# Hybrid decoder layer: the mLSTM convolutions placed with the output gate's units, and the last two pairs of down sums moved into the down projection

## The chip, the cores and the metric

The kernel runs on one core of one Trainium2 chip. The metric is the device time of one execution in microseconds (us), as the median over runs. The engines are PE (matmuls), DVE, ACT, POOL (elementwise work) and SP, whose queue issues nearly all transfers between HBM and on-chip memory. Each engine takes its instructions in the order in which they were written into its stream, and stands still at one whose operands are not there.

## The reference

One layer of a decoder trunk in float32, sequence 1024, width 1024. One input projection feeds a differential-attention group and an mLSTM group; their outputs go through an output projection; a gated MLP (inner width 2816) with a width-3 convolution follows.

```python
hn = rmsnorm(x, attn_norm_w)
da_q, da_k, da_v, ml_qk, ml_v, ml_o, ml_i, ml_f = split_projection(hn @ w_in)
...
qk = silu(causal_dwconv(ml_qk, mlstm_conv_w, mlstm_conv_b))      # width 4, 1024 channels
mq, mk = split(qk)
i_pre, logf = ml_i + igate_b, log_sigmoid(ml_f + fgate_b)
h = rmsnorm(mlstm_chunkwise(mq, mk * 128 ** -0.5, ml_v, i_pre, logf))
ml_out = sigmoid(ml_o) * h
x = x + concat([da_out, ml_out]) @ w_out
u = causal_dwconv(rmsnorm(x) @ w_up, ffn_conv_w, ffn_conv_b)
gate, up = split(u)
x = x + (silu(gate) * up) @ w_down
out = rmsnorm(x)
```

## The kernel before

**Arithmetic.** Every float32 matrix is split into a high and a low part: ACT copies it rounded (L112), DVE or POOL subtracts that from the source (L113, the same shape). A product is then three matmuls (L155 to L157 with moving x, L160 to L162 with moving weights). Up and down projections are done by a scheme that uses seven products of half-size blocks instead of eight, with sums of blocks as operands.

**First projections.** Eight column tiles `ct` of the convolved half (mq is 0 to 3, mk 4 to 7) are projected first, each in two halves of 512 positions. A half ends with ACT's copy out of PSUM (L376, L390) into `mqk`, and DVE multiplies the whole tile by the norm's row `RB` (L384, L391). `conv_qk(ct)` makes the width-4 convolution: one ACT instruction (L358) and three DVE instructions of some 1,022 columns (L360), into a tile tagged `ta` (four buffers). `silu_qk(ct)` is one ACT instruction (L363). Behind the column tiles PE does the gate projection, 16 matmuls per half (L408), each half in a PSUM bank tagged `sa` or `sb` and copied out by DVE (L409). Then come the output gate's units, `o_unit(tt)`, 24 matmuls for 128 positions each with the four pieces of weights `wo`, and the same with `wv` in `v_unit(tt)`, mixed with the small work on the gates (L474 transposes them).

**Down sums.** The seven-product scheme needs sums of blocks of `w_down`. They depend on weights alone, so they are made early: `down_sums` loads a pair of row blocks, POOL makes four subtractions of 128x512 in place (L324), and `store_sums` writes the pair to `wsum` in HBM (L330). There are 11 pairs. `late_sums` does the same in the `ta` tiles. Two pairs of up sums follow in `first_up_sums`.

**Down projection.** PE makes 77 steps, seven products (order 1, 2, 7, 5, 6, 4, 3) of 11 steps i, 12 matmuls a step. Ahead of step k `dprep_to(k + 5)` prepares operands: some products need sums of activation blocks (L1153, DVE), each step needs two splits, one of activations (`hb`, `a`) and one of weights (tiles `wf` and `bw`, loaded two steps at a time, from `w_down` in products 1, 2 and 3 and from `wsum` in 7, 5, 6 and 4). A finished product is added into the `x2` tiles (L1194, DVE). `fill(k)` issues the loads that belong to step k: activation blocks `a21`, `a12`, `a22`, the residual tiles `x2[0..3]` at steps 8 to 11 and `x2[4..7]` at 20 to 26, and the final norm's row `fin` at 19.

**Order.** The text of the program is not the order of an engine. A scheduler places each instruction by when its inputs are expected, so two texts can give one order, and a load can move ahead of others on SP. SP has one queue: a store that waits for POOL holds up the weights behind it.

Of the kernel before, what the change touches and what calls it, by code (L numbers as in the profile page):

```python
# [13 lines left out]
AF = mybir.ActivationFunctionType  # L14
ALU = mybir.AluOpType
# [9 lines left out]
NJ = DFF // P  # L25
# [14 lines left out]
def tile_hybrid(ctx: ExitStack, tc: tile.TileContext, I: dict, out: bass.AP):  # L40
    nc = tc.nc
    V = nc.vector
    A = nc.scalar
    PE = nc.tensor
    GP = nc.gpsimd
# [61 lines left out]
    wsum = dp.tile([NJ // 2, 2, P, 1024], F32, name="wsum")  # L107
# [13 lines left out]
    HV = (slice(0, 512), slice(512, 1024))  # L121
# [50 lines left out]
    def small(shape):  # L172

        flip[0] ^= 1
        return psA.t(shape, tag="sa" if flip[0] else "sb")
# [7 lines left out]
    def rotate(n):  # L183
        return (mmps, lambda: big([P, 512]), lambda: small([P, 512]))[n % 3]()
# [12 lines left out]
    def load_x(i, hf, between=None):  # L197
        f = pa.t(XS, tag="ta", bufs=4)
        for c in ([slice(0, 1), slice(1, 2)] if between else [slice(0, 2)]):
            nc.sync.dma_start(f[:, c, :], I["xT"][:, 2 * i + c.start:2 * i + c.stop, HV[hf]])  # L200
            if between and c.start == 0:
                between()
        return f
# [41 lines left out]
    def col_piece(ct):  # L245
        cw[ct, 0], cw[ct, 1] = wpiece(I["w_st"][ct], None, V)

    g0 = col_halves(0, 0, 1, first=True)
    f = load_x(0, 0, lambda: next(g0))
    next(g0)  # L250
    split_x(0, 0, f)
    f = load_x(1, 0)
# [5 lines left out]
    f = load_x(2, 0)  # L258
# [3 lines left out]
    f = load_x(3, 0)  # L262
# [5 lines left out]
    for i in range(4):  # L268
        f = load_x(i, 1)
# [39 lines left out]
    gs = pa.t([16, S], tag="gs")  # L309
# [1 line left out]


    dsum = []
    pairs = list(range(NJ // 2))

    def down_sums(alloc=lambda: pr0.t([P, S], tag="vda", bufs=4), n=1):
        h0, h1 = HV
        for i in (pairs.pop(0) for _ in range(min(n, len(pairs)))):
            g, u = (alloc() for _ in range(2))
            for k, f in enumerate((g, u)):  # L320
                nc.sync.dma_start(f, I["w_down"][2 * i + k])
            for dst, x_, y in ((g[:, h1], g[:, h1], g[:, h0]), (u[:, h1], u[:, h1], g[:, h1]),
                               (u[:, h0], u[:, h0], u[:, h1]), (g[:, h0], u[:, h1], g[:, h0])):
                GP.tensor_tensor(dst, x_, y, op=ALU.subtract)  # L324
            dsum.append((i, g, u))

    def store_sums(n=1):
        for i, g, u in (dsum.pop(0) for _ in range(min(n, len(dsum)))):
            for k, f in enumerate((g, u)):
                nc.sync.dma_start(usum[i - NJ, k] if i >= NJ else wsum[i, k], f)  # L330
# [13 lines left out]
    def tok(tiles, tt):  # L344
        return tiles[tt // 2][:, tt % 2, :]

    def col_mm(ps, ct, kc, hf):
        k = slice(kc % 4 * P, (kc % 4 + 1) * P)
        w = cw[ct, kc // 4]
        mm3(ps, w[:, 0, k], w[:, 1, k], *xpart(kc, hf), kc == 0, kc == KC - 1)  # L350
# [3 lines left out]
    def conv_qk(ct):  # L354

        u = M[ct]
        acc = cacc[ct] = pa.t([P, S], tag="ta", bufs=4)
        A.activation(acc, u, AF.Identity, bias=mcb[:, ct:ct + 1], scale=mcw[:, ct, 3:4])  # L358
        for d in (1, 2, 3):
            V.scalar_tensor_tensor(acc[:, d:], u[:, :S - d], mcw[:, ct, 3 - d:4 - d], acc[:, d:], op0=ALU.mult, op1=ALU.add)  # L360

    def silu_qk(ct):
        A.activation(M[ct], cacc.pop(ct), AF.Silu)  # L363
# [21 lines left out]
    for ct in range(4, 8):  # L385
        for hf in range(2):
            ps = rotate(2 * ct + hf)
            for kc in range(KC):
                col_mm(ps, ct, kc, hf)
            A.activation(M[ct][:, HV[hf]], ps, AF.Copy)  # L390
        V.tensor_tensor(M[ct], M[ct], RB, op=ALU.mult)  # L391
        store_sums()
        down_sums()
        if ct == 4:
            col_piece(7)
        elif ct == 6:
            wo = [getw(0) for _ in range(4)]
        conv_qk(ct - 4)
        if ct > 4:
            silu_qk(ct - 5)  # L400
    mq, mk = M[0:4], M[4:8]


    for hf in range(2):
        gp = small([16, 512])
        for kc in range(KC):
            for m, x_ in enumerate(xpart(kc, hf)):
                PE.matmul(gp, wg16[:, kc, :], x_, start=(kc, m) == (0, 0), stop=(kc, m) == (KC - 1, 1))  # L408
        V.tensor_copy(gs[:, HV[hf]], gp)  # L409
    conv_qk(4)  # L410
    silu_qk(3)

    def mv_mm(ps, w, tt):
        for kc in range(KC):
# [6 lines left out]
    def late_sums():  # L421
        store_sums()
        down_sums(lambda: pa.t([P, S], tag="ta", bufs=4))
# [7 lines left out]

    def o_unit(tt):
        store_sums()
        if tt < 4:
            if tt < 3:
                conv_qk(5 + tt)
            silu_qk(4 + tt)
        if tt % 2:
            late_sums()
        if tt == 5:  # L440
            wv.extend(getw(0) for _ in range(4))
        if tt == NT - 1:
            return
        tts = (tt,) if tt < NT - 2 else (tt, tt + 1)
        pss = [rotate(k) for k in tts]
        mv_pair(pss, wo, tts)
        for ps, k in zip(pss, tts):
            A.activation(tok(Tt, k), ps, AF.Tanh, scale=rstdh[:, k:k + 1])

    def v_unit(tt):  # L450
        store_sums()
        if tt in (2, 4):
            first_up_sums(tt // 2 - 1)
        if tt == 0:
            late_sums()
            vda.extend(pr0.t([P, 2, 512], tag="vda", bufs=4) for _ in range(4))
        if tt == NT - 1:
            return
        tts = (tt,) if tt < NT - 2 else (tt, tt + 1)
        pss = [rotate(k + 2) for k in tts]  # L460
        mv_pair(pss, wv, tts)
        for ps, k in zip(pss, tts):
            A.activation(tok(vda, k), ps, AF.Copy, scale=rstd[:, k:k + 1])
# [325 lines left out]
    x2 = []  # L789
# [326 lines left out]
    def weights(p, i):  # L1116
        if i % 2 == 0:
            wload(p, i)
        return wb.pop((p, i))

    def fill(k):

        if k == 2:
            load(a21[:, 0:4, :], "A21", (0, 4))
        elif k == 4:
            load(a12, "A12", (4, NP - 1))
        elif k == 6:
            load(a21[:, 4:8, :], "A21", (4, 8))
        elif k in (8, 9, 10, 11):
            nc.sync.dma_start(x2[k - 8], x2d[k - 8])  # L1130
        elif k == 12:
            load(a21[:, 8:, :], "A21", (8, NP))
            load(a12[:, NP - 5:, :], "A12", (NP - 1, NP))
        elif k == 13:
            load(a22[:, 0:6, :], "A22", (0, 6))
        elif k == 17:
            load(a22[:, 6:, :], "A22", (6, NP))
        elif k in (20, 22, 24, 26):
            tt = 4 + (k - 20) // 2
            nc.sync.dma_start(x2[tt], x2d[tt])  # L1140
        elif k == 19:
            nc.sync.dma_start(fin, I["final_norm"].partition_broadcast(P))
            V.tensor_scalar(fin, fin, RSC, None, op0=ALU.mult)
# [40 lines left out]
    x2 = [pd.t([P, D], tag="x2", bufs=8) for _ in range(NT)]  # L1184
# [69 lines left out]
    k = 0  # L1254
# [95 lines left out]
```

## Time and profile before

| quantity | value |
|---|---|
| median of 3 runs | 1224.06 us (1218.65 to 1227.42) |
| the profiled execution's own time | 1228.44 us |
| its span in the profile | 1226.6 us |
| busy PE, DVE, ACT, POOL | 1196.3, 898.2, 572.6, 475.5 us |
| mean granted PE clock | 0.994 |
| down projection, first matmul | 1006.64 us |

Times in the profile count from the span's start; 1.8 us of the execution lie outside the span. `PEclk` or "granted clock" is the share of full speed that PE was granted. A row of a timeline gives start, duration, engine, line, operation, output and input tiles, shape, count, and in brackets the idle time ahead of it with what ended it.

### The profile page before, as it was taken

Reading aid. Unit: us, or ns where it says so; the run is one execution under the profiler, and the core shown is the slowest. Engines: PE = TensorE matmul, PEld = TensorE weight load, DVE = VectorE, ACT = ScalarE, POOL = GpSimd, SP = SyncE. Lnnn points to the kernel's source line nnn. Section 1 sums busy time; section 2 is a strip of 40 time slices with the busy share of each in tenths; the row PEclk is TensorE's granted clock in tenths of the full one; section 3 lists DMA queues with packets and bytes.
Section 4 is the critical chain, followed back from the end, with each engine's and each line's share of the span. In section 5 each row is a group of like instructions: output and inputs, shape, how many; then the busy total and the mean of one; then the engine's idle time right before and its main releaser. Section 6 shows DMA issues by size and latency. Waiting matters only on the chain.

```text
span 1226.6 us, 15935 instructions
## 1 busy us (share of the span) xinstructions
PE 1196.3 (98%) x5622; PEld 977.0 (80%) x5622; DVE 898.2 (73%) x1564; ACT 572.6 (47%) x1114; POOL 475.5 (39%) x364
## 2 busy tenths in 40 slices
PE   9998999999999999999999999999999999999996
PEld 7885788888778878888888888888888888888885
DVE  5598232566767777669998878787787768896694
ACT  6533323333666665444643443434344445544462
POOL 0475441003543431001398878786877600000000
PEclk9998999999999999999999999999999999999999
DMA  8755564114212252432222222222222158832323
GB/s 304 257 207 196 216 240 164 61 70 158 75 54 51 69 167 100 138 129 99 99 69 103 86 102 70 86 69 86 80 76 101 54 207 321 308 106 96 95 78 137
DMA packets 61744, 159.03 MB, mean 130 GB/s; under 512 B 6177, under 2 KB 10465, under 8 KB 61665
## 3 DMA queue, kind: packets, MB, share of 16 engines
q1 hardware_dynamic: 61232, 157.21, 37.3%
q8 instruction: 44, 0.72, 0.2%
q10 hardware_dynamic: 432, 0.82, 0.2%
q14 instruction: 36, 0.29, 0.1%
HBM read 116.02 MB, written 37.78 MB: 125 GB/s over the span
## 4 chain that ended last, share of the span: by engine, by line
PE 80%; DMA 5%; DVE 5%; ACT 3%; POOL 3%; issue 2%; SPq 1%; POOLq 0%; ACTq 0%; DVEq 0%
PE mm L155 6%; PE mm L157 6%; PE mm L156 5%; PE mm L160 5%; PE mm L162 4%; PE mm L161 4%; PE big L155 4%; PE big L157 4%; PE big L156 4%; PE big L160 4%; PE big L162 4%; PE big L161 4%; PE sb L769 3%; POOL vda L324 3%; PE sb L155 2%
## 5 line engine op out<-in xcount | busy, mean ns | idle before, releaser
L112 ACT ACTIVATE w<-wf 128x512 fp32r<-128x512 f32 x160 | 97.8, 624 | 137.4 <-PE mm L157 33.7
L113 DVE TENSOR_TENSOR w<-wf,w 128x512 fp32r<-128x512 f32 x128 | 109.6, 868 | 24.1 <-ACT w L112 18.7
L1033 DVE SCALAR_TENSOR_TENSOR y<-x2b,fcw,y 128x1022 f32<-128x1022 f32 x44 | 89.6, 2076 | 0.0
L1032 DVE SCALAR_TENSOR_TENSOR y<-x2b,fcw,y 128x1023 f32<-128x1023 f32 x44 | 71.3, 1660 | 10.4 <-ACT y L1031 10.4
L324 POOL TENSOR_TENSOR vda<-vda 128x512 f32<-128x512 f32 x24 | 47.1, 1978 | 63.3 <-DMA vda<-in_w_down_dram 62.4
L113 POOL TENSOR_TENSOR w<-s,w 128x512 fp32r<-128x512 f32 x40 | 68.3, 1706 | 7.1 <-ACT w L112 7.1
L113 POOL TENSOR_TENSOR w<-wf,w 128x512 fp32r<-128x512 f32 x32 | 46.2, 1449 | 62.4 <-ACT w L112 50.2
L113 POOL TENSOR_TENSOR w<-wu,w 128x512 fp32r<-128x512 f32 x40 | 67.4, 1685 | 2.9 <-ACT w L112 2.9
L155 PE MATMUL mm<-xb,w 128*128 128x512 f32 x168 | 66.4, 395 | 0.0
L157 PE MATMUL mm<-xb,w 128*128 128x512 f32 x168 | 65.9, 392 | 0.0
L156 PE MATMUL mm<-xb,w 128*128 128x512 f32 x168 | 65.9, 392 | 0.0
L744 DVE CUSTOM_DVE_ANT_0 s<-big,B 128x128 f32<-128x128 f32 (+7 forms) x64 | 47.6, 754 | 14.0 <-PE big L742 12.6
L1031 ACT ACTIVATE y<-x2b,fcw 128x1024 f32<-128x1024 f32 x44 | 52.3, 1237 | 11.2 <-DVE x2b L1022 9.8
L746 ACT ACTIVATE s<-s,mb 128x128 f32<-128x128 f32 (+7 forms) x64 | 49.3, 772 | 11.5 <-DVE mb L745 10.4
L112 ACT ACTIVATE w<-s 128x512 fp32r<-128x512 f32 x43 | 27.0, 629 | 55.1 <-PE mm L157 18.6
L160 PE MATMUL big<-w 128*128 128x512 f32 x132 | 51.5, 390 | 0.8 <-DVE x L1194 0.8
L960 POOL TENSOR_TENSOR s<-wu 128x512 f32<-128x512 f32 x20 | 31.2, 1562 | 54.2 <-DMA wu<-in_w_up_dram 54.2
L162 PE MATMUL big<-w 128*128 128x512 f32 x132 | 51.4, 389 | 0.0
L161 PE MATMUL big<-w 128*128 128x512 f32 x132 | 51.4, 389 | 0.0
L112 ACT ACTIVATE w<-wu 128x512 fp32r<-128x512 f32 x48 | 29.8, 627 | 43.6 <-PE mm L157 13.4
L1022 DVE TENSOR_TENSOR x2b<-x2b,big 128x512 f32<-128x512 f32 x53 | 35.4, 680 | 20.0 <-PE big L157 19.2
L1022 DVE TENSOR_TENSOR x2b<-x2b,mm 128x512 f32<-128x512 f32 x51 | 34.1, 681 | 21.4 <-PE mm L157 20.6
(514 smaller groups left out, 3802.0 us busy)
## 6 DMA issues: line engine op xcount, KB each, us to landing
wf<-in_w_up_dram SPq DMA_DIRECT2D x22, 512.0 KB, 4.4
actd<-y SPq DMA_DIRECT2D x21, 512.0 KB, 2.6
wu<-in_w_up_dram SPq DMA_DIRECT2D x20, 512.0 KB, 3.5
wf<-in_w_st_dram SPq DMA_DIRECT2D x12, 512.0 KB, 4.2
vda<-in_w_down_dram SPq DMA_DIRECT2D x12, 512.0 KB, 5.9
wsum<-vda SPq DMA_DIRECT2D x12, 512.0 KB, 3.1
wf<-in_w_mv_dram SPq DMA_DIRECT2D x12, 512.0 KB, 5.3
wf<-wsum SPq DMA_DIRECT2D x12, 512.0 KB, 3.4
```

Of the source, the lines that this page charges most:

```text
L112: A.activation(dst[:, 0, :], src, AF.Copy)
L113: loeng.tensor_tensor(dst[:, 1, :], src, dst[:, 0, :].bitcast(F32), op=ALU.subtract)
L155: PE.matmul(ps, sh, mh, start=first, stop=False)
L156: PE.matmul(ps, sh, ml, start=False, stop=False)
L157: PE.matmul(ps, sl, mh, start=False, stop=last)
L160: PE.matmul(ps, sh, w[:, 0, :], start=first, stop=False)
L161: PE.matmul(ps, sl, w[:, 0, :], start=False, stop=False)
L162: PE.matmul(ps, sh, w[:, 1, :], start=False, stop=last)
L324: GP.tensor_tensor(dst, x_, y, op=ALU.subtract)
L1022: V.tensor_tensor(dst, src, ps, op=ALU.add)
L1032: V.scalar_tensor_tensor(y[:, 1:], u[:, :S - 1], cw[:, 1:2], y[:, 1:], op0=ALU.mult, op1=ALU.add)
L1033: V.scalar_tensor_tensor(y[:, 2:], u[:, :S - 2], cw[:, 0:1], y[:, 2:], op0=ALU.mult, op1=ALU.add)
```

## The change

Three things move.

The first projections make down sums in `ct` 5 and 7 only (besides 1 and 3 of the first half), and the convolutions stand one tile to three tiles later in the text: tile `ct - 5` in the loop, tiles 3 to 7 in `o_unit(0..4)`. The gates are copied out of PSUM by ACT instead of DVE.

The two last pairs of down sums (9 and 10) leave the first projections. `fill` makes them in the down projection: at steps 14 and 15 it loads them into the tiles of `x2[4..7]`, POOL subtracts, at steps 18 and 20 they are stored to `wsum`, and the residual is loaded into those tiles two steps later than before. Product 7, the first that reads `wsum`, begins at step 22; its pair 8 and 9 is loaded for step 30.

`late_sums` in the v units moves from unit 0 to 2, and the up sums from 2 and 4 to 3 and 5.

```diff
-    pairs = list(range(NJ // 2))
+    pairs = list(range(NJ // 2 - 2))
+
+    def pair_sums(g, u):
+        h0, h1 = HV
+        for dst, x_, y in ((g[:, h1], g[:, h1], g[:, h0]), (u[:, h1], u[:, h1], g[:, h1]),
+                           (u[:, h0], u[:, h0], u[:, h1]), (g[:, h0], u[:, h1], g[:, h0])):
+            GP.tensor_tensor(dst, x_, y, op=ALU.subtract)
...
         V.tensor_tensor(M[ct], M[ct], RB, op=ALU.mult)
-        store_sums()
-        down_sums()
+        if ct % 2:
+            store_sums()
+            down_sums()
...
-        conv_qk(ct - 4)
         if ct > 4:
-            silu_qk(ct - 5)
+            conv_qk(ct - 5)
+        if ct > 5:
+            silu_qk(ct - 6)
...
-        V.tensor_copy(gs[:, HV[hf]], gp)
-    conv_qk(4)
-    silu_qk(3)
+        A.activation(gs[:, HV[hf]], gp, AF.Copy)
...
     def o_unit(tt):
         store_sums()
-        if tt < 4:
-            if tt < 3:
-                conv_qk(5 + tt)
-            silu_qk(4 + tt)
         if tt % 2:
             late_sums()
+        if tt < 5:
+            conv_qk(3 + tt)
+        if tt < 6:
+            silu_qk(2 + tt)
...
+    def last_sums(i, g, u):
+
+        for m, f in enumerate((g, u)):
+            nc.sync.dma_start(f, I["w_down"][2 * i + m])
+        pair_sums(g, u)
+
     def fill(k):
...
+        elif k in (14, 15):
+            last_sums(k - 5, x2[2 * k - 24], x2[2 * k - 23])
+        elif k in (18, 20):
+            i = k // 2
+            for m in range(2):
+                nc.sync.dma_start(wsum[i, m], x2[2 * i - 14 + m])
-        elif k in (20, 22, 24, 26):
-            tt = 4 + (k - 20) // 2
+        elif k in (22, 24, 26, 28):
+            tt = 4 + (k - 22) // 2
             nc.sync.dma_start(x2[tt], x2d[tt])
```

**SP in the first projections.** These are the rows of SP's queue from the weights of column tile 7 (`wf<-in_w_st`) to the last two of the four `wo` loads (`wf<-in_w_mv`); `vda` and `ta` loads are pairs of down sums, two rows a pair, and `wsum<-vda` stores one. Before:

```order
L126 DMA wf<-in_w_st_dram 128x1024
L330 DMA wsum<-vda 128x1024 x2
L321 DMA vda<-in_w_down_dram 128x1024 x4
L330 DMA wsum<-vda 128x1024 x2
L126 DMA wf<-in_w_mv_dram 128x1024 x2
L330 DMA wsum<-vda 128x1024 x2
L126 DMA wf<-in_w_mv_dram 128x1024 x2
```

Now, over the same stretch:

```order
L126 DMA wf<-in_w_st_dram 128x1024
L326 DMA vda<-in_w_down_dram 128x1024
L333 DMA wsum<-vda 128x1024 x2
L326 DMA vda<-in_w_down_dram 128x1024
L126 DMA wf<-in_w_mv_dram 128x1024 x2
L333 DMA wsum<-vda 128x1024 x2
L326 DMA vda<-in_w_down_dram 128x1024 x2
L126 DMA wf<-in_w_mv_dram 128x1024
L326 DMA ta<-in_w_down_dram 128x1024
L333 DMA wsum<-vda 128x1024 x2
L326 DMA ta<-in_w_down_dram 128x1024
L126 DMA wf<-in_w_mv_dram 128x1024
```

The first two `wo` loads stand behind the stores of pairs 0 and 1 instead of 0 to 3, the third behind 0 to 2 and the fourth behind 0 to 3, instead of 0 to 4 for both.

**ACT around the gate projection.** The rows from the second half of column tile 6 on (`mqk_254` is that tile, `mqk_253` and `mqk_255` the ones beside it; `sa` is the PSUM bank that the gates' second half needs). Before:

```order
L390 ACTIVATE mqk_254<-big_718 128x512
L112 ACTIVATE w_776<-wf_771 128x512
L363 ACTIVATE mqk_253<-ta_906 128x1024
L358 ACTIVATE ta_938<-mqk_254,par_67 128x1024
L390 ACTIVATE mqk_255<-sa_793 128x512
L363 ACTIVATE mqk_254<-ta_938 128x1024
L112 ACTIVATE w_781<-wf_779 128x512
L112 ACTIVATE w_784<-wf_779 128x512
L390 ACTIVATE mqk_255<-mm_819 128x512
L358 ACTIVATE ta_1003<-mqk_255,par_67 128x1024
L363 ACTIVATE mqk_255<-ta_1003 128x1024
```

Now:

```order
L393 ACTIVATE mqk_254<-big_702 128x512
L112 ACTIVATE w_750<-wf_745 128x512
L366 ACTIVATE mqk_253<-ta_971 128x1024
L361 ACTIVATE ta_1011<-mqk_254,par_67 128x1024
L393 ACTIVATE mqk_255<-sa_767 128x512
L366 ACTIVATE mqk_254<-ta_1011 128x1024
L112 ACTIVATE w_755<-wf_753 128x512
L112 ACTIVATE w_758<-wf_753 128x512
L393 ACTIVATE mqk_255<-mm_793 128x512
L361 ACTIVATE ta_1045<-mqk_255,par_67 128x1024
L414 ACTIVATE gs_260<-sb_836 16x512
L414 ACTIVATE gs_260<-sa_854 16x512
```

The order is the same up to the two gate copies, which are new on ACT and stand ahead of the last silu. On DVE the 24 convolution instructions also still stand ahead of the first work on the gates, and 18 of them ahead of the product of `mqk_254` with `RB`, as before.

**DVE in the down projection, second product.** The rows from step 19 on (`w2_9173` and `w2_9174` are its two splits before, `w2_9159` and `w2_9160` now; `a21<-a21,a22` is a block sum). Before:

```order
L113 TENSOR_TENSOR w2_9173<-a12_8828,w2_9173 128x512
L113 TENSOR_TENSOR w_9194<-a12_8828,w_9194 128x512
L1153 TENSOR_TENSOR a21_8829<-a21_8829,a22_8830 128x512 x4
L113 TENSOR_TENSOR w2_9174<-wf_9175,w2_9174 128x512
L113 TENSOR_TENSOR w_9195<-wf_9175,w_9195 128x512
L113 TENSOR_TENSOR w_9213<-a12_8828,w_9213 128x512
L113 TENSOR_TENSOR w_9214<-bw_9215,w_9214 128x512
L113 TENSOR_TENSOR w_9235<-hb_8707,w_9235 128x512
L1153 TENSOR_TENSOR a21_8829<-a21_8829,a22_8830 128x512 x6
L113 TENSOR_TENSOR w_9236<-wf_9237,w_9236 128x512
```

Now (from the third row on):

```order
L1169 TENSOR_TENSOR a21_8809<-a21_8809,a22_8810 128x512 x6
L113 TENSOR_TENSOR w2_9160<-wf_9161,w2_9160 128x512
L113 TENSOR_TENSOR w_9187<-wf_9161,w_9187 128x512
L113 TENSOR_TENSOR w_9205<-a12_8808,w_9205 128x512
L113 TENSOR_TENSOR w_9206<-bw_9207,w_9206 128x512
L113 TENSOR_TENSOR w_9227<-hb_8687,w_9227 128x512
L113 TENSOR_TENSOR w2_9271<-hb_8687,w2_9271 128x512
L1169 TENSOR_TENSOR hb_8687<-a22_8810,hb_8687 128x512 x2
L1210 TENSOR_TENSOR x2_8811<-x2_8811,mm_9060 128x512
L1210 TENSOR_TENSOR x2_8812<-x2_8812,mm_9061 128x512
L1210 TENSOR_TENSOR x2_8813<-x2_8813,sb_9062 128x512
L1210 TENSOR_TENSOR x2_8814<-x2_8814,sa_9063 128x512
```

Six block sums instead of four stand ahead of step 19's weights, and the four additions of the finished second product stand ahead of `w_9228`, step 22's weights, which follow them by one block sum (`w_9236` is the same split before). On SP the four new loads (L1128) stand between the first load of `a22` and its second one, the weights of steps 19 and 20 behind the first two of them and those of step 21 behind all four; the stores (L1153) stand behind step 22's weights, two ahead of `fin`, two ahead of the weights of step 26.

More of the change, by code (lines that the diff above doesn't have):

```diff
@@ L313, in tile_hybrid @@
     dsum = []
-    pairs = list(range(NJ // 2))
+    pairs = list(range(NJ // 2 - 2))
[4 more added lines that the diff above has]
+            GP.tensor_tensor(dst, x_, y, op=ALU.subtract)
     def down_sums(alloc=lambda: pr0.t([P, S], tag="vda", bufs=4), n=1):
-        h0, h1 = HV
         for i in (pairs.pop(0) for _ in range(min(n, len(pairs)))):
@@ L321, in down_sums @@
                 nc.sync.dma_start(f, I["w_down"][2 * i + k])
-            for dst, x_, y in ((g[:, h1], g[:, h1], g[:, h0]), (u[:, h1], u[:, h1], g[:, h1]),
-                               (u[:, h0], u[:, h0], u[:, h1]), (g[:, h0], u[:, h1], g[:, h0])):
-                GP.tensor_tensor(dst, x_, y, op=ALU.subtract)
+            pair_sums(g, u)
             dsum.append((i, g, u))
@@ L451, in v_unit @@
         store_sums()
-        if tt in (2, 4):
+        if tt == 2:
+            late_sums()
+        if tt in (3, 5):
             first_up_sums(tt // 2 - 1)
         if tt == 0:
-            late_sums()
             vda.extend(pr0.t([P, 2, 512], tag="vda", bufs=4) for _ in range(4))
@@ L1119, in weights @@
         return wb.pop((p, i))
+    def last_sums(i, g, u):
+        for m, f in enumerate((g, u)):
+            nc.sync.dma_start(f, I["w_down"][2 * i + m])
+        pair_sums(g, u)
     def fill(k):
```

## The prediction

> **What bounds the kernel now.** I read the engine table first, then the waits of PE, then stretches of time around them.
>
> ```profile
> PE 1196.3 (98%) x5622; PEld 977.0 (80%) x5622; DVE 898.2 (73%) x1564; ACT 572.6 (47%) x1114; POOL 475.5 (39%) x364
> ...
> PE sa L408 <- ACT mqk L390: 5.9, 1, 5.9
> ...
> PE big L600 <- DVE kw L597: 3.1, 3, 1.4
> ...
> PE sb L474 <- DVE gs L409: 2.5, 1, 2.5
> ```
>
> PE is busy for all but 30 us of 1226.6, so an edit off PE is worth only a PE wait that it removes or makes. The first and third wait are the ones this change can reach: the gate projection (L408) waits for a PSUM bank that ACT empties late, and the gates' transposes (L474) wait for DVE's copy of them. Their stretch in PE's timeline and in windows (columns: length, busy PE, PEld, DVE, ACT, POOL, granted clock, DMA share, GB/s):
>
> ```profile
> 96.12 3.87 PE L408 MATMUL sb<-xb,wg 128*16 128x512 f32 x16
> 105.94 5.57 PE L408 MATMUL sa<-xb,wg 128*16 128x512 f32 x16 [5.94 <-ACT mqk L390]
> ...
> 106.00:110.00 4.00, 4.00 (x11) 1.33 (x12) 3.96 (x2) 0.00 (x0) 3.92 (x3) 0.54 0.00 0
> ...
> 122.00:126.00 4.00, 1.49 (x12) 0.99 (x11) 3.46 (x4) 1.30 (x2) 1.53 (x1) 1.00 0.78 271
> 126.00:130.00 4.00, 4.00 (x13) 3.11 (x12) 0.95 (x6) 3.94 (x6) 1.37 (x2) 0.59 0.98 362
> ```
>
> The first wait costs 5.94 us, and the same sixteen matmuls then take 5.57 us instead of 3.87: 1.70 more at a clock of 0.54. The second costs 2.51 us, and 4 us at a clock of 0.59 lose 4 x 0.41 = 1.64. Together 11.8 us, just under 1% of the run: the front cannot give more.
>
> **Why the first wait stands where it does.** ACT empties the bank (L390, mqk<-sa) in its order, behind a convolution's first part (L358), which needs DVE's L391:
>
> ```profile
> 104.16 1.24 ACT L358 ACTIVATE ta<-mqk,par 128x1024 f32<-128x1024 f32 x1
> 105.31 0.58 ACT L390 ACTIVATE mqk<-sa 128x512 f32<-128x512 f32 x1
> ...
> 53.54 6.84 DVE L384 TENSOR_TENSOR mqk<-mqk,RB 128x1024 f32<-128x1024 f32 x4 [2.44 <-ACT RB L299]
> ...
> 101.10 0.69 DVE L113 TENSOR_TENSOR w<-wf,w 128x512 fp32r<-128x512 f32 x1 [0.78 <-ACT w L112]
> 102.91 1.22 DVE L391 TENSOR_TENSOR mqk<-mqk,RB 128x1024 f32<-128x1024 f32 x1
> 104.04 1.75 DVE L113 TENSOR_TENSOR w<-wf,w 128x512 fp32r<-128x512 f32 x1
> ```
>
> From 53.54 to 102.91 DVE pauses once that matters, 0.78 us, when a wo half arrived late through ACT. So DVE's work sets the bank's release. That work is stretched by POOL: the split at 104.04, beside POOL, took 1.75 where the one at 101.10, with POOL idle, took 0.69. Each POOL turn costs DVE 1.06 us.
>
> **The change, front part.** The program moves three convolutions later, but the order built from it does not: DVE still has 18 convolution steps, the same splits and the same products ahead of the sixth column tile's product, and ACT still empties the bank behind that convolution. What counts is then how many POOL turns fall before 102.91. Before:
>
> ```profile
> 55.20 15.26 POOL L324 TENSOR_TENSOR vda<-vda 128x512 f32<-128x512 f32 x7 [4.65 <-DMA vda<-in_w_down_dram]
> 77.12 16.67 POOL L324 TENSOR_TENSOR vda<-vda 128x512 f32<-128x512 f32 x8 [6.65 <-DMA vda<-in_w_down_dram]
> ...
> 59.33 2.56 SPq L330 DMA_DIRECT2D wsum<-vda  x2
> 71.34 3.98 SPq L321 DMA_DIRECT2D vda<-in_w_down_dram  x4
> ```
>
> That is 7 + 8 = 15 turns. After, SP issues the second tile of pair 2 behind pair 1's stores (61.9), pair 3 behind pair 2's, the second tile of pair 4 behind pair 3's. A load takes some 5.8 us to POOL (71.34 to 77.12), a turn 2.1 (16.67 / 8). So pair 2 ends at 61.9 + 5.8 + 3 x 2.1 = 74, pair 3 at 74 + 5.8 + 8.4 = 88, pair 4 at 88 + 5.8 + 6.3 = 100: with the rest of pair 1 (3 turns) 15 turns again. DVE gains only its 0.78 us pause, because wo's loads now stand behind fewer stores. **First wait: 5.9 becomes 5.1, its clock loss stays: -0.8.**
>
> The second wait goes. Its cover is these rows:
>
> ```profile
> 114.18 1.29 DVE L113 TENSOR_TENSOR w<-wf,w 128x512 fp32r<-128x512 f32 x2 [1.71 <-ACT w L112]
> 124.53 0.67 DVE L409 COPY gs<-sa 16x512 f32<-16x512 f32 x1
> ...
> 116.64 1.24 ACT L358 ACTIVATE ta<-mqk,par 128x1024 f32<-128x1024 f32 x1 [1.49 <-DVE mqk L391]
> ```
>
> The gates' last copy, on DVE behind three convolution steps, ended at 125.2. Now both stand on ACT behind the last L358 (117.9) and take 0.6 each: 119.1, less the 0.8. PE asks for them after two units of 24 matmuls of 0.227 us ((1066.52 - 1058.36) / 36 by the PE rows further down), at 110.5 + 10.9 = 121.4. That gives 2.51 + 1.64: **-4.2**. Late next is wo's last quarter, on DVE at 115.5 - 0.8 = 114.7, where PE wants its first half 18 matmuls into the unit, at 110.5 + 4.1 = 114.6: no new wait, by a hair.
>
> Behind 130 us POOL and SP have less to do than before. Conv 6's tile now waits for pair 4's stores (100, and some 3 to land), with the bank's release queued behind it on ACT: that is level with L391's 102, so up to 1 us of the gain can go there. Front: **-5.0**.
>
> [...]
>
> **The change, down projection.** Eight POOL operations of a stage that had none, and 4 loads and 4 stores of 512 KB. Here I looked at DMA, then at DVE's lead over PE:
>
> ```profile
> 1020.00:1050.00 30.00, 30.00 (x134) 24.82 (x134) 23.23 (x38) 13.94 (x25) 0.00 (x0) 1.00 1.04 391
> 1050.00:1062.00 12.00, 12.00 (x55) 9.94 (x54) 10.94 (x19) 5.87 (x11) 0.00 (x0) 1.00 1.05 396
> 1062.00:1080.00 18.00, 18.00 (x81) 14.92 (x80) 17.52 (x30) 10.03 (x21) 0.00 (x0) 1.00 0.44 155
> ...
> a<-actd SPq DMA_DIRECT2D x1, 1536.0 KB, 14.2
> ...
> wf<-in_w_down_dram SPq DMA_DIRECT2D x1, 512.0 KB, 14.2
> ```
>
> DMA is full until 1062 (share 1.04, 391 GB/s), so transfers land in order, 1.34 us per 512 KB. a22's first load, issued at 1034.7, lands at 1048.9; pair 9 is next and lands at 1050.2 and 1051.6; the weights of step 19 (the step of i = 8 in the second product) land at 1052.9 instead of 1050.2; pair 10 lands at 1054.3 and 1055.6. POOL then runs from 1050 to about 1063. In just that stretch DVE works without a pause:
>
> ```profile
> 1051.06 0.69 DVE L113 TENSOR_TENSOR w<-a,w 128x512 fp32r<-128x512 f32 x1 [2.03 <-ACT w L112]
> 1051.67 2.49 DVE L1153 TENSOR_TENSOR a<-a,a 128x512 f32<-128x512 f32 x4
> 1054.08 1.28 DVE L113 TENSOR_TENSOR w<-wf,w 128x512 fp32r<-128x512 f32 x2
> ...
> 1058.36 0.39 PE L160 MATMUL mm<-w,w 128*128 128x512 f32 x1
> ...
> 1066.52 0.39 PE L160 MATMUL big<-w 128*128 128x512 f32 x1
> ```
>
> The split at 1054.08 is step 19's, done at 1054.8; PE starts that step at 1058.36: a lead of 3.6 us. After the change six sums (L1169, L1153 before) stand ahead of it instead of four: 2 x 0.6 = 1.2, lead 2.4. And of POOL's eight turns seven fall between 1051 and that split, since DVE has eight operations there and the two engines take turns: 7 x 1.06 = 7.4. Step 19 is late by **+5.0**, and the clock's price of a wait of that length is that of the 5.94 us one, **+1.7**.
>
> A new wait follows at step 22, the first of the third product. Four additions that need PE's second product (L1210) now stand on DVE ahead of its weights' split; before, that split was done at 1061.4, 5 us ahead of 1066.52. After PE's last matmul of the second product DVE still has one addition, one sum and the split, 0.6 + 0.6 + 0.7, and the step's third matmul is the first that needs it (0.45 later): **+1.4**, with no clock loss: L600's waits of 1.4 us and less (second wait of the first fence) left it at 1.00 here:
>
> ```profile
> 220.00:240.00 20.00, 19.07 (x131) 17.01 (x131) 13.62 (x42) 8.13 (x36) 0.11 (x1) 1.00 0.19 60
> ```
>
>  Behind pair 9's stores on SP stand fin (final_norm's row, for which DVE waits ahead of step 24's weights) and the weights themselves; behind pair 10's, step 26's.
>
> ```profile
> 1042.77 4.17 SPq L1142 DMA_DIRECT2D fin<-in_final_norm_dram  x1
> ...
> fin<-in_final_norm_dram SPq DMA_DIRECT2D x1, 512.0 KB, 14.2
> ```
>
> Pair 9's last turn ends near 1057, so fin is issued at 1058 and lands by 1065 (in order, behind 2 stores) to 1072 (by its own 14.2); DVE wants it, 3.2 us ahead of step 24 (1071.96 + 6.7 of delay), at 1075.5: hidden. The last four x2 tiles are not needed before step 43. Down: **+8.1**, with bounds of 0, if POOL's turns fall into DVE's pauses (1.1 and 2.0 us near 1050), and 12, if all eight turns fall on it, a second clock loss follows and fin is late as well.
>
> **Sum.** -5.0 + 8.1 = +3.1 on the profiled execution's 1228.44 us, which is 0.36% above the median of the runs; on that median, 1224.06, it is 1227.2. I say **1227 us**: slower by 0.25%, which a measurement here cannot tell from no change, for 1% (12 us) is about what it can.
>
> **Rivals.** (A) The lead holds: POOL's loads land early, in DVE's pauses, or its turns bite less on in-place sums; the down projection costs 0 to 3, the total is -5 to -2, 1219 to 1222. For it, most steps lead by over 7 us; against it, step 19's 3.6. (B) The front's first wait goes too, because pair 4 slips behind 103 and takes four turns (4.2 us) with it, and the clock stays up: -11.8 in front, with +8 in the down part 1220, with nothing there 1212. Against it, SP's order has pair 4's loads around pair 3's stores. (C) Slower: fin. If DMA is still full when it is issued (4 loads and 4 stores add 8 x 1.34 = 10.7 us to that stretch) and pair 9's last turn ends after 1061, 4 us later than worked out, DVE stands at fin with step 24's weights behind it, and each us more is one of PE. It needs loads that land later or turns of 2.1 us instead of 1.7; 3 to 9 us on top of the forecast give 1230 to 1236. (D) The change does not do what it says: for the convolutions I already count it so.
>
> **From this to the numbers.** Forecast (+0 to +6) 0.50, A 0.24, B 0.14, C 0.12. The runs of one kernel spread by 0.36% either way, so I widen by 3: the range is 1216 to 1233. Faster by over 1% needs B with nothing lost behind it, 0.05; slower by over 1%, the far end of C, 0.06; within 1%, 0.89.
>
> **What would show it.** In the changed profile: L413 in sa waits about 5 us for ACT, with the clock near 0.5 behind it; the wait of the gates' transposes on the copy is gone; eight POOL operations named x near 1045 to 1060 with DVE's sums of 512 columns at about 1.7 us beside them; a PE wait of about 5 us in mm for DVE or ACT, and a short one at the first matmul in big. I am wrong if the wait at L413 is under 2 us, or if PE stays at full count through the second product.

## The result, and the profile after

The changed kernel ran at 1.005 times the time of the kernel before, 95% interval 1.0029 to 1.0072: 6.1 us slower, 3.5 to 8.8. The medians of nine runs each are 1234.77 us (1228.74 to 1235.75) and 1224.06 us (1218.65 to 1231.55). The run times of both kernels fall into two groups, 5.6 and 5.8 us apart by the groups' medians, two against seven runs after and five against four before, so their medians differ by more than the ratio says (the last section has two paces of one stage that lie, by an estimate, about as far apart); the ratio puts the change at 1230 us on the median of before, inside the range, while the median of nine itself lies 1.8 us above it. The profiled execution took 1235.59 us, 7.15 more than that of before.

The page after begins with its span and busy times, and PE's waits are these (total, times, longest):

```profile
span 1233.5 us, 15943 instructions
...
PE 1199.6 (97%) x5622; PEld 978.5 (79%) x5622; DVE 902.4 (73%) x1562; ACT 573.3 (46%) x1116; POOL 477.2 (39%) x364
```

```profile
PE mm L162 <- DVE w L113: 5.4, 1, 5.4
PE sa L413 <- ACT mqk L393: 5.1, 1, 5.1
...
PE big L160 <- ACT w L112: 0.8, 1, 0.8
```

The gate projection's wait (L408 before, L413 now) is 5.1 instead of 5.9, the wait of the gates' transposes is gone, and a new wait of 5.4 stands in mm, the second product of the down projection. PE executes the same 5622 matmuls in the same order in both kernels, so the start of each can be compared, and the shift shows where time went (here and below, times such as 13 or 130 us are those of the kernel before, and the shift is that of a matmul next to them):

| up to | shift, after minus before | this stage alone |
|---|---|---|
| 13 us, first matmuls | +1.6 | +1.6 (the code there is the same) |
| gate projection done | +0.8 | -0.8 |
| 130 us | -3.5 | -4.3 |
| 1058 us | -3.2 | +0.3 |
| third matmul of step 19 | +2.4 | +5.6 |
| end of the second product | +4.9 | +2.5 |
| step 24, and so to the end | +6.8 | +2.0 |

In the front, the two windows of 4 us in which PE had waited and run at 0.59 are full now, at full clock (columns as in the prediction):

```profile
122.00:126.00 4.00, 4.00 (x24) 3.12 (x23) 2.06 (x4) 3.10 (x4) 3.84 (x4) 1.00 0.01 3
126.00:130.00 4.00, 4.00 (x20) 3.30 (x19) 1.66 (x4) 2.42 (x4) 1.11 (x1) 1.00 0.76 282
```

In the down projection, the timelines of POOL, DVE and PE stand one above the other:

```profile
1047.46 1.30 POOL L320 TENSOR_TENSOR x<-x 128x512 f32<-128x512 f32 x1 [64.20 <-DMA x<-in_w_down_dram]
...
1058.86 1.70 POOL L320 TENSOR_TENSOR x<-x,x 128x512 f32<-128x512 f32 x1
```

```profile
1047.82 1.49 DVE L113 TENSOR_TENSOR w<-a,w 128x512 fp32r<-128x512 f32 x1 [2.03 <-ACT w L112]
1049.23 10.21 DVE L1169 TENSOR_TENSOR a<-a,a 128x512 f32<-128x512 f32 x6
1059.37 2.35 DVE L113 TENSOR_TENSOR w<-wf,w 128x512 fp32r<-128x512 f32 x2
```

```profile
1061.17 0.80 PE L162 MATMUL mm<-w,w 128*128 128x512 f32 x1 [5.43 <-DVE w L113]
...
1072.35 0.50 PE L160 MATMUL big<-w 128*128 128x512 f32 x1 [0.77 <-ACT w L112]
```

POOL's eight subtractions run from 1047.46 to 1060.56. DVE's six sums beside them take 10.21 us, 1.70 each, where four took 2.49 before, and step 19's split behind them ends at 1061.1; PE resumes at 1061.17. The clock behind that wait and before it:

```profile
1056.00:1060.00 4.00, 0.00 (x0) 0.00 (x0) 4.00 (x4) 0.00 (x0) 3.92 (x3) 0.93 0.95 351
1060.00:1066.00 6.00, 4.83 (x11) 3.80 (x12) 3.52 (x5) 0.16 (x1) 0.57 (x1) 0.50 0.99 351
```

### The profile page after: what moved, and what is told of

Read it like the earlier page. It is cut to its first block, busy times and chain, and to the rows that moved or that the text cites. A ratio compares the mean times of both kernels' runs of the same rounds, so it can differ in the third digit from the quotient of the medians.

```text
span 1233.5 us, 15943 instructions
## 1 busy us (share of the span) xinstructions
PE 1199.6 (97%) x5622; PEld 978.5 (79%) x5622; DVE 902.4 (73%) x1562; ACT 573.3 (46%) x1116; POOL 477.2 (39%) x364
## 4 chain that ended last, share of the span: by engine, by line
PE 83%; DVE 8%; ACT 3%; issue 3%; DMA 2%; POOL 0%; SPq 0%; POOLq 0%; DVEq 0%; ACTq 0%
PE mm L155 6%; PE mm L157 6%; PE mm L156 6%; PE big L155 5%; PE big L157 5%; PE big L156 5%; PE mm L160 4%; PE mm L162 4%; PE mm L161 4%; PE big L162 4%; PE big L161 4%; PE big L160 4%; PE sb L773 3%; PE sb L155 2%; PE sa L155 2%
## 5 line engine op out<-in xcount | busy, mean ns | idle before, releaser
L113 DVE TENSOR_TENSOR w<-wf,w 128x512 fp32r<-128x512 f32 x128 | 106.4, 841 | 21.0 <-ACT w L112 16.8
L750 ACT ACTIVATE s<-s,mb 128x128 f32<-128x128 f32 (+7 forms) x64 | 49.3, 772 | 11.5 <-DVE mb L749 10.4
L320 POOL TENSOR_TENSOR vda<-vda 128x512 f32<-128x512 f32 x16 | 31.1, 1955 | 55.0 <-DMA vda<-in_w_down_dram 51.7
L320 POOL TENSOR_TENSOR ta<-ta 128x512 f32<-128x512 f32 x20 | 32.9, 1653 | 47.9 <-DMA ta<-in_w_down_dram 47.4
L162 PE MATMUL big<-w 128*128 128x512 f32 x132 | 51.3, 390 | 0.0
```

The lines of the kernel that those rows point to most:

```text
L113: loeng.tensor_tensor(dst[:, 1, :], src, dst[:, 0, :].bitcast(F32), op=ALU.subtract)
L162: PE.matmul(ps, sh, w[:, 1, :], start=False, stop=last)
```

## The experiments

Every experiment is read by the shift of its matmuls, stage by stage, in its trace, and by its ratio to before where one is given; the others have the one profiled execution alone.

**The down projection: POOL's turns or the transfers?** Two kernels leave out subtractions and keep loads, stores and every engine's order. The first leaves out all eight:

```diff
     for m, f in enumerate((g, u)):
         nc.sync.dma_start(f, I["w_down"][2 * i + m])
-    pair_sums(g, u)
+    pass
```

> The changed kernel with the eight POOL subtractions of the down projection left out (pairs 9 and 10 are stored as loaded); the four loads, the four stores and each engine's order stay. Theory: DVE's work ahead of step 19's weights is slowed by POOL's turns alone; without them PE's wait in the second product goes from 5.4 us to 0 and the clock stays up, so the down projection's delay falls from 9.9 to at most 2 us and the run ends some 8 us earlier than the changed kernel. The short wait at the third product stays at about 1 us, since it comes from the four additions that stand ahead of the split. Rival: the loads and stores (DMA full to 1062, the queue's order) make step 19 late; then 3 us or more of the wait stay.

DVE's timeline at the same place:

```profile
1043.80 3.70 DVE L1169 TENSOR_TENSOR a<-a,a 128x512 f32<-128x512 f32 x6
1047.41 1.29 DVE L113 TENSOR_TENSOR w<-wf,w 128x512 fp32r<-128x512 f32 x2
```

The same six sums took 3.70 us instead of 10.21, that is 1.09 less for each, PE's wait was gone and the clock stayed at 1.00 between 1056 and 1066. The down projection cost 2.0 us instead of 10.1; 0.77 us of wait at the third product's first matmul stayed, as expected. All loads and stores were there, so the transfers by themselves cost PE nothing at step 19.

The second keeps pair 9's four:

```diff
-    pair_sums(g, u)
+    i == 9 and pair_sums(g, u)
```

> The changed kernel with POOL's subtractions of pair 10 left out and the four of pair 9 kept; loads, stores and order stay. Theory: each POOL turn costs DVE 1.06 us, the four that go are the last four of eight that fell ahead of step 19's split, so the wait of 5.4 us becomes 5.4 - 4.2 = 1.2 us, and a wait that short leaves the clock up: the run ends 6 to 7 us earlier than the changed kernel. Rival: the wait is set by when transfers land: it stays above 3 us.

```profile
1057.20 0.50 PE L162 MATMUL mm<-w,w 128*128 128x512 f32 x1 [1.17 <-DVE w L113]
```

1.17 us, against 1.2 worked out, at a clock of 1.00 between 1056 and 1066; the down projection cost 3.5 us instead of 10.1. Both waits give the same lead of step 19: 8 x 1.06 - 5.43 and 4 x 1.06 - 1.17 are both 3.1 us. In both runs the wait is the number of turns times 1.06, less that lead.

**The same eight turns at another place.** The two pairs are loaded at steps 3 and 5.

```diff
-        elif k in (14, 15):
-            last_sums(k - 5, x2[2 * k - 24], x2[2 * k - 23])
+        elif k in (3, 5):
+            last_sums((k + 15) // 2, x2[k + 1], x2[k + 2])
```

> The changed kernel with the last two pairs' loads issued at steps 3 and 5 of the down projection instead of 14 and 15; the same eight POOL turns, then at about 1018 to 1034 us. Theory: a turn costs DVE the same 1.06 us there, but the steps it prepares lead PE by 5 to 9 us and DVE pauses in between, so PE waits 0 to 1.5 us in the second product instead of 5.4, and the clock stays up. Rival 1: the cost is one of the turns themselves, wherever they stand, and PE waits 5 us elsewhere in the first or second product. Rival 2: the four loads ahead of the activations' loads make these late, and PE waits for them near steps 4 to 12.

The wait at step 19 went, but three others came, in the first product and at the start of the second, of 1.24, 1.30 and 1.75 us; the down projection cost 5.2 us instead of 10.1. ACT's timeline shows what the first of them waited for. In this run:

```profile
1030.04 0.63 ACT L112 ACTIVATE w<-hb 128x512 fp32r<-128x512 f32 x1 [10.25 <-PE big L162]
1030.58 0.61 ACT L112 ACTIVATE w<-bw 128x512 fp32r<-128x512 f32 x1
```

In the changed kernel:

```profile
1024.55 0.63 ACT L112 ACTIVATE w<-bw 128x512 fp32r<-128x512 f32 x1 [3.96 <-DMA bw<-in_w_down_dram]
1025.09 0.62 ACT L112 ACTIVATE w<-hb 128x512 fp32r<-128x512 f32 x1
```

The `bw` row is the weights of step 10, which PE waited for until 1031.24. Their load, issued at 1017.49 behind the four new ones, took 11.8 us and landed at 1029.33. But they now stand behind the split of an activation block, and that one waited until PE had ended step 9, at 1030.00; in the changed kernel the weights stand ahead. So moving the loads also changed ACT's order (and DVE's, in the same way), and this run gives a price neither for the turns nor for the loads at this place. My expectation of 0 to 1.5 us was wrong, and my second rival, that the loads make the wait, is not shown.

**One part at a time.** The kernel before with the moved pairs alone, the rest of its front unchanged (the diff is the down projection's part of the change, with `pairs` two shorter):

```diff
-    pairs = list(range(NJ // 2))
+    pairs = list(range(NJ // 2 - 2))
...
+        elif k in (14, 15):
+            last_sums(k - 5, x2[2 * k - 24], x2[2 * k - 23])
```

> The kernel before with the two last pairs of down sums moved into the down projection and nothing else: same loops of the first projections, same convolutions, gates copied by DVE. Theory: the down projection is late by what the changed kernel shows, 5.4 us of wait in the second product, 2.4 us by the low clock behind it, and 1 to 2 us at the third product, together +9 to +10 us, and the front is as before, both waits there: ratio 1.008. Rival: the front gains too, since the sums end earlier there, and the total is +5 or less (1.004 or under).

Ratio 1.0084 (1.0054 to 1.0114), +10.3 us. The wait in mm was 5.5 us, and the down projection's shift +10.4. In the front both waits were there, 7.2 and 1.9 us, the second without a fall of the clock (1.00 from 122 to 130).

And the gates' copies alone:

```diff
-        V.tensor_copy(gs[:, HV[hf]], gp)
+        A.activation(gs[:, HV[hf]], gp, AF.Copy)
```

> The kernel before with one edit: the gates' two copies out of PSUM on ACT. Theory (the prediction's): the wait of the gates' transposes on that copy goes, 2.5 us of idle PE and the 1.6 us that the low clock behind it costs, -4.2 us in all, and the whole front gain but 0.8 us belongs to this edit; the wait for the PSUM bank ahead of it stays at 5.9 us. Ratio to before 0.9966. Rival 1: the clock does not fall for a wait of 2.5 us by itself, and only 2.5 us come back (0.998). Rival 2: without the convolutions and sums moved, ACT's copies stand behind later convolution work, and PE still waits 1 us or more for them (0.998 to 1.000).

Ratio 0.9974 (0.9955 to 0.9993), -3.2 us. By the matmuls' starts, -4.3 us between the gate projection and 130 us; the second wait was gone, the clock 1.00 from 122 to 130, and the bank's wait stayed at 6.1. So the front's gain is this edit but for the 0.8 us of the first wait; the two parts sum to +7 by these ratios, and the whole measured +6.1.

**Why the first wait stands.** The convolutions go back to their old place in the text, all else as changed:

```diff
-        if ct > 4:
-            conv_qk(ct - 5)
-        if ct > 5:
-            silu_qk(ct - 6)
+        conv_qk(ct - 4)
+        if ct > 4:
+            silu_qk(ct - 5)
...
-        if tt < 5:
-            conv_qk(3 + tt)
-        if tt < 6:
-            silu_qk(2 + tt)
+        tt < 3 and conv_qk(5 + tt)
+        tt < 4 and silu_qk(4 + tt)
```

> The changed kernel with the convolutions and silus where the text of before had them; the rest of the change stays. On DVE and ACT the order is nearly the same, but the convolutions hold the four ta tiles longer, so pair 4's loads stand behind the last of the output gate's weights and its four POOL turns fall behind the sixth column tile's product. Theory: four turns fewer ahead of it, 4.2 us, so the gate projection's wait falls from 5.1 to about 1 us. Rival: if moving the convolutions had any worth of its own, as a change of DVE's order, the wait is the 5.9 us of before or longer. Down projection as in the changed kernel.

```profile
101.94 5.46 PE L413 MATMUL sa<-xb,wg 128*16 128x512 f32 x16 [1.93 <-ACT mqk L393]
```

The wait fell from 5.06 to 1.93 us, and between 13 and 130 us this kernel gained 8.4 us where the changed one gained 5.1. So the convolutions' new place cost 3.3 us, by a side effect: it frees the `ta` tiles early, and the scheduler fills them with pair 4's loads, whose turns then stand ahead of the product that PE waits for (here three of the four come behind it). Next, the changed kernel with the subtractions of pairs 2 to 4 left out:

```diff
-            pair_sums(g, u)
+            i in (2, 3, 4) or pair_sums(g, u)
```

> The changed kernel with POOL's subtractions of pairs 2, 3 and 4 left out in the first projections (twelve turns that fell between 57 and 98 us); loads, stores and order stay. Theory: DVE reaches the sixth column tile's product 12.7 us earlier, the gate projection's wait of 5.1 us is gone, and the clock stays up behind it: 6.8 us less by the end of the gate projection. Rival: the wait is set by ACT's order or by transfers; 3 us or more of it stay.

The wait was gone, and the shift between 13 us and the end of the gate projection was 7.0 us better; DVE and ACT keep their order, on SP a few rows change places. Four traces now give the price of a turn. Each line is the window from DVE's first product with `RB` to that of the sixth column tile; DVE does the same 31 instructions in it, its busy time is the third of the busy times, and POOL's count stands behind the last. This one is of the kernel with pairs 2 to 4 left out:

```profile
54.12:90.92 36.80, 36.80 (x164) 30.49 (x163) 36.01 (x31) 21.16 (x26) 6.94 (x4) 1.00 0.80 288
```

with the convolutions back,

```profile
53.56:98.91 45.35, 45.35 (x201) 36.29 (x200) 45.35 (x31) 21.02 (x26) 25.32 (x12) 1.00 0.52 187
```

the changed kernel,

```profile
55.14:103.58 48.44, 46.45 (x205) 36.59 (x203) 48.40 (x31) 21.24 (x26) 30.91 (x16) 1.00 0.61 218
```

and the kernel before (its count of 32 takes in the product with which the window ends):

```profile
53.54:102.91 49.37, 46.45 (x205) 36.60 (x203) 48.48 (x32) 21.07 (x26) 31.39 (x15) 1.00 0.62 223
```

Two of POOL's counts take in a turn that only begins as the window ends: the fourth of the first line starts at 90.69, the sixteenth of the third at 103.45. With 3, 12, 15 and 15 turns DVE's busy time grows from 36.01 to 45.35, 48.40 and 48.48 us, 1.03 to 1.04 for a turn. The change had left the turns where they were, 15 as before, and took only DVE's pauses, 0.9 us before and next to none after.

**A front with fewer turns.** The kernel before, with the gates' copies on ACT and the down sums of column tiles 5 to 7 moved into the units:

```diff
         store_sums()
-        down_sums()
+        ct == 4 and down_sums()
...
-        if tt % 2:
+        if tt:
             late_sums()
```

> The kernel before with two edits: the gates' copies on ACT, and down sums taken out of the loop over column tiles 5 to 7 and made in the output gate's units 1 to 7 and in v unit 0 instead (all 11 pairs stay in the first projections, the down projection is that of before). Theory: DVE's product of the sixth column tile, which the bank's release stands behind, is late by 1.06 us for every POOL turn ahead of it; 7 turns are left there instead of 15, so it comes 8.5 us earlier, the 5.9 us wait for the bank and the 1.7 us of low clock behind it go, and with the gates' copies on ACT the 2.5 + 1.6 us go too: -10 to -12 us, ratio 0.990 to 0.992, provided that the output gate's weights are split by then (they stand behind fewer stores). Rival 1: the bank waits for something else (ACT's own order), and 4 us or more of the first wait stay: ratio 0.995 to 0.997, as the gates' copies alone. Rival 2: the sums that move into the units hold up the v weights on SP's queue or run past the units' end, and a new wait of 3 us or more between 130 and 200 us takes the gain.

Ratio 0.9985 (0.9963 to 1.0007). With 8 turns the window above was 42.86 us long, both waits were gone and by 130 us the matmuls were 11.8 us ahead. Then 6.3 us went by 170 us, 3.4 of them by the clock (0.50 from 157.69 to 164.51), and by 575 only 3.2 were left. PE's and SP's timelines:

```profile
155.13 0.50 PE L162 MATMUL sa<-w,xb 128*128 128x512 f32 x1 [0.72 <-DVE w L113]
...
157.49 0.64 PE L160 MATMUL sa<-w,xb 128*128 128x512 f32 x1 [1.86 <-ACT w L112]
```

```profile
134.42 6.77 SPq L330 DMA_DIRECT2D wsum<-ta  x4
142.35 2.04 SPq L321 DMA_DIRECT2D ta<-in_w_down_dram  x3
144.50 0.37 SPq L126 DMA_DIRECT2D wf<-in_w_mv_dram  x1
151.61 0.33 SPq L330 DMA_DIRECT2D wsum<-ta  x1
152.03 0.38 SPq L126 DMA_DIRECT2D wf<-in_w_mv_dram  x1
```

The v weights (`wf`) stand behind stores that wait for POOL, and are issued late, at 144.50 and 152.03: my second rival. Two gentler versions put the moved sums later:

```diff
-        down_sums()
+        ct % 2 and down_sums()
...
-        if tt in (2, 4):
-            first_up_sums(tt // 2 - 1)
-        if tt == 0:
+        if tt in (3, 5):
+            first_up_sums((3, 5).index(tt))
+        if tt in (0, 1, 2):
             late_sums()
```

> The kernel before with the gates' copies on ACT, down sums in the loop only in column tiles 5 and 7, in the output gate's units 1, 3, 5 and 7 and in the v units 0, 1 and 2, and the up sums in v units 3 and 5; all 11 pairs stay in the first projections and the down projection is that of before. Theory: eleven POOL turns instead of fifteen fall ahead of the sixth column tile's product, so the first wait falls from 5.9 to about 2 us with one window of low clock (1.7), the second goes: -8 us by 130 us; SP's order as far as the v weights is that of the kernel whose v units had no wait, so the v weights come in time, and two pairs more follow them. Ratio 0.993 to 0.995. Rival: the pairs that now end later hold up the gates' transfers behind them on SP's queue, and 3 us or more are lost between 150 and 310 us: ratio 0.997 or more.

```diff
-        down_sums()
+        ct != 6 and down_sums()
...
-        if tt == 0:
+        if tt in (0, 1):
             late_sums()
```

> The kernel before with the gates' copies on ACT and one pair of down sums moved out of column tile 6's place in the loop into v unit 1; all else as before. Theory: about eleven POOL turns fall ahead of the sixth column tile's product, the first wait falls to 2 us or less, the second goes, -8 us by 130 us, and with one pair moved instead of three the v units lose less than 2 of it: ratio 0.993 to 0.995. Rival: as for the other, 3 us or more are lost behind the v weights: 0.997 or more.

Both missed: 1.0019 (0.9997 to 1.0041) and 1.0015 (0.9995 to 1.0034). The first was 8.0 us ahead at 130 us, and lost 8.8 between 203 and 213, where the last weights of that stage stood behind the up sums' stores on SP's queue:

```profile
188.85 8.95 SPq L330 DMA_DIRECT2D usum<-ta  x4
197.85 0.42 SPq L126 DMA_DIRECT2D wf<-in_w_mv_dram  x1
```
 
The second did not even do its front part: the scheduler let the next pair's loads take the freed `vda` tiles, 15 turns were left where I had worked out 11, and the bank's wait was 5.3 us. It too lost 6.1 us between 203 and 213, and the last version below, whose stores are on another queue, lost 5.0 there; so what those stores have to do with that loss is argued here and not shown.

So the stores were taken off SP's queue, with the front of eight turns:

```diff
-                nc.sync.dma_start(usum[i - NJ, k] if i >= NJ else wsum[i, k], f)
+                (GP if i > 2 else nc.sync).dma_start(usum[i - NJ, k] if i >= NJ else wsum[i, k], f)
```

> The kernel with eight POOL turns ahead of the sixth column tile's product (gates' copies on ACT, down sums in column tile 4 and then in the output gate's units 1 to 7 and v unit 0), whose front gained 11.7 us by 130 us and lost 6 behind 155, with one further edit: the sums of pairs 3 to 10 and the up sums are stored by POOL's own DMA queue, right behind the subtractions, instead of by SP's. Theory: the v weights came late since they stood behind those stores on SP's queue, which wait for POOL; without them the wait at 155 us goes and at least 8 of the 11.7 us stay: ratio 0.991 to 0.994. Rival 1: the loads of the sums still stand on SP's queue and wait for the stores to land, so the wait stays: 0.998. Rival 2: issuing from POOL costs POOL and DVE more than SP's wait, and the units become slower: 1.000 or more.

```profile
146.93 1.39 SPq L126 DMA_DIRECT2D wf<-in_w_mv_dram  x2
```

The v weights are issued at 146.9 together, the waits at 155 to 158 us shrink to 0.46 and 1.16 without a fall of the clock (1.00 from 134 to 160), and the ratio is **0.9937 (0.9916 to 0.9958)**, 7.7 us faster than before: this version beats both kernels. With the loads on POOL's queue too,

```diff
-                nc.sync.dma_start(f, I["w_down"][2 * i + k])
+                (GP if i > 2 else nc.sync).dma_start(f, I["w_down"][2 * i + k])
```

> As the one with the stores on POOL's queue, and the loads of pairs 3 to 10 on POOL's queue too, so that SP's queue carries only weights and the gates' transfers in that stretch. Theory: no weight waits for a sum any more, 8 us or more of the 11.7 us gained by 130 us stay: ratio 0.991 to 0.994. Rival: the sums now run one behind the other on POOL, end later than 200 us, and the work that waits for POOL or for the four tiles behind them takes 5 us or more: 0.997 or more.

it was 1.0037 (1.0017 to 1.0058): 11.7 us ahead at 130 us, and 3.4 behind at 310, with waits of 3.4 us for DVE near 142 and four, 3.7 in all, for the weights' splits, and a mean clock of 0.994 over the execution, against 0.997 with the stores alone moved. In the text a pair's load now stands on POOL behind the pair before it, as the rival had it; which of the waits follows from that was not tried.

## Why the prediction was right, and where it was off

- **First wait, -0.8:** the wait fell by 0.9 (5.94 to 5.06) and the stage by 0.8, for the reason given: the 15 turns that I worked out were 15, and DVE's pause went. The four traces with this front have 5.0 to 5.3 us here, the three with the order of before 5.9 to 7.2.
- **Second wait, -4.2:** measured -4.3, and -4.3 with that edit alone.
- **Late next:** wo's last quarter made no wait, and the front as a whole, -5.0, measured -5.1.
- **Step 19, +5.0:** +5.6, of which 5.43 is the wait. A turn's 1.06 us was right. The landing times were not: I had pair 9 land at 1050.2 and step 19's weights at 1052.9; POOL began at 1047.46, and ACT split those weights at 1049.98:

```profile
1049.98 1.16 ACT L112 ACTIVATE w<-wf 128x512 fp32r<-128x512 f32 x2 [2.19 <-DMA wf<-in_w_down_dram]
```

  All eight turns therefore fell ahead of the end of the split, not seven, and the lead was 3.1 us, not 2.4. Of those 0.7 us 0.45 are plain from the row of the wait: the step's third matmul (L162) is the first that needs the split, and I had counted from its first. The two errors nearly cancel, so that the term came out this close is in part luck.
- **The clock behind it, +1.7:** +2.5. This term was mis-sized: I took the loss of the 5.94 us wait, but two whole windows of low clock, less 1.7 us of idle time in them, stood here (below).
- **Third product, +1.4:** +2.0. The matmuls at the 0.77 us wait lost the 1.4; another 0.5 went at step 24, where DVE had no lead left, which I had not counted. From 1072 to 1090 it was busy without a pause (third of the busy times):

```profile
1072.00:1079.00 7.00, 6.64 (x28) 5.10 (x28) 7.00 (x13) 4.76 (x11) 0.00 (x0) 1.00 0.40 145
1079.00:1090.00 11.00, 10.75 (x48) 8.64 (x47) 11.00 (x19) 6.07 (x12) 0.00 (x0) 1.00 0.45 147
```

- **fin hidden:** yes; it was issued at 1054.75, 3 us earlier than worked out, and nothing waited for it. Rival C did not come, nor A (the lead did not hold), nor B (the first wait stayed).
- **Sum:** -5.1 + 0.3 + 10.1 = +5.3 where I had +3.1, and the profiled execution lost another 1.6 us in its first 13 us, with the same code. The gap of the sum lies in the down projection, 10.1 for 8.1, inside its bounds of 0 and 12. The sign held; that the loss would be too small to measure did not, since the eighteen runs put it clear of zero.

## What to carry to other kernels

Count, for every engine that feeds the bottleneck, the turns of another engine that slows it, up to the instruction that is waited for: here a POOL subtraction beside DVE cost 1.0 to 1.1 us wherever DVE had no slack, and the same eight of them, moved from the front into the down projection, cost 10.3 us. Moving text under a scheduler can move buffers and loads while the engines' work stays in order, so read which buffers come free. Keep a store that waits for a slow engine from standing ahead of weights: on that engine's own queue the stores turned 0.9985 into 0.9937 here, while moving the loads there as well gave 1.0037.

## What the runs showed of the hardware

**The clock fell by windows.** In the traces of the kernel before and of the changed one, low clock came in stretches of 3.41 or 6.83 us (but for the last one, which the end cuts off), at a granted clock of 0.50, and their starts lie whole multiples of 3.413 us apart: 102.86, 126.75 and 1222.43 us before, 8.17, 103.74, 1059.47 and 1226.72 us after. Cut on that grid, the kernel before shows around its second wait

```profile
123.34:126.75 3.41, 1.49 (x9) 1.27 (x10) 2.80 (x6) 2.05 (x3) 0.19 (x1) 1.00 0.74 229
126.75:130.17 3.42, 3.42 (x10) 2.67 (x9) 0.45 (x4) 3.34 (x6) 1.53 (x2) 0.50 1.02 387
130.17:133.58 3.41, 3.41 (x17) 2.78 (x16) 1.07 (x1) 1.67 (x2) 3.33 (x3) 1.00 0.45 183
```

and the changed kernel around step 19

```profile
1056.06:1059.47 3.41, 0.00 (x0) 0.00 (x0) 3.41 (x4) 0.00 (x0) 3.33 (x3) 1.00 0.92 357
1059.47:1062.89 3.42, 1.72 (x4) 1.44 (x5) 3.42 (x5) 0.00 (x0) 1.10 (x1) 0.50 1.00 364
1062.89:1066.30 3.41, 3.41 (x9) 2.64 (x9) 0.63 (x2) 0.46 (x1) 0.00 (x0) 0.50 1.01 336
1066.30:1069.71 3.41, 3.41 (x16) 2.79 (x16) 2.03 (x4) 0.17 (x1) 0.00 (x0) 1.00 1.03 407
```

In these two traces every window at half speed stood behind one in which PE was idle for 1.53 us or more. Behind a window that ran at full speed, idle times of 1.92, 2.15, 2.52, 2.86 and 3.41 us were always followed by half speed, 1.39 us and less never, and between them it went either way: 1.53 us was (4.75 to 8.16, changed kernel), 1.44 and 1.66 us were not (355.45 to 358.86 and 1215.61 to 1219.02, before). Behind a window already at half speed, 1.69 us was enough in the second line of the changed kernel, and none at all, by PE's records, in the kernel with eight turns from 157.69 to 161.10, where the clock was still 0.50 between 161 and 164; what decides there is open. So the price of a wait hung on where it fell on the grid: the wait of 1.93 us with the convolutions back cost a window (the sixteen matmuls behind it took 5.46 us, not 3.87; the mean clock from 50 to 108 us was 0.97), while the second wait of the pairs alone, 1.86 us, fell on two windows (1.07 and 0.79) and cost none. The 1.6 us at the start of the profiled execution are in the main such a window, from 8.17 to 11.58, at 0.50.

**A POOL subtraction held up a DVE sum.** In the changed kernel a sum took 1.70 us beside POOL (10.21 / 6), and 0.62 with the subtractions left out (3.70 / 6). The two engines went one for one there: POOL's eight subtractions from 1047.46 to 1060.56, DVE's eight instructions beside them from 1047.82 to 1061.1.

**The up projection ran at two paces.** Between 700 and 900 us, PE without a pause, the kernel before executed 858 matmuls in its profile, and the kernel with the gates' copies alone 871:

```profile
700.00:900.00 200.00, 200.00 (x858) 161.84 (x857) 159.21 (x144) 83.38 (x112) 155.70 (x94) 1.00 0.23 79
```

```profile
700.00:900.00 200.00, 200.00 (x871) 163.15 (x870) 165.27 (x148) 82.95 (x114) 163.29 (x97) 1.00 0.24 82
```

That is 233 or 230 ns a matmul at the same granted clock of 1.00, 3.0 us for the 13 matmuls more in these 200 us; over the stage's 1858 matmuls (575 to 1006.64 us before) it would be 6.5 us, an estimate from these two counts. The changed kernel's trace has 858 in this window too, that of the version with the stores on POOL's queue 871. The edits leave this stage alone, so it seems a matter of the execution and not of the kernel; but the same program was not profiled at both paces, and what sets the pace is open.
